# Average pooling of a 3D tensor: another cut of the rows into partitions, and one ring buffer for all loads

## The chip, the core and the metric

The kernel runs on one core of a Trainium2 chip. The metric is the device time of one execution in microseconds, as the median of several runs. Most runs of one kernel lie within a fraction of a per cent of each other.

## The reference

The input `x` is float32 of shape (8, 32, 32, 32, 32): 256 channels (batch times channel), each a cube of 32 x 32 x 32. With kernel size 2 every cube of 2 x 2 x 2 is replaced by its mean:

```
result[:, :, i, j, k] = mean(x[:, :, 2i:2i+2, 2j:2j+2, 2k:2k+2], axis=(-3, -2, -1))
```

The output is (8, 32, 16, 16, 16). 33.55 MB are read and 4.19 MB are written, and each input is used once. One *plane pair*, two neighbouring planes of 32 x 32 along the depth, is 2048 floats (8 KB) of contiguous memory and gives one output plane of 16 x 16, 256 floats (1 KB). There are 4096 such pairs, and in memory they follow each other without a gap, in the output too.

## The kernel before

`pool_rows` works on 128 partitions. The 256 channels are taken as two halves, `t` = 0 and 1: partition p holds channel p of the half. A channel is 128 KB of input and 16 KB of output, so rows of neighbouring partitions lie 128 KB apart in the input and 16 KB apart in the output. `KF` is 256 floats, 1 KB; positions and lengths in the code (`k0`, `kb`) count in KB per partition.

`plan` (L42) lists the loads. There are six of 32 KB per partition (4 MiB for all partitions), and the last two entries are cut into two loads of 16 KB each, so ten in all. Each entry takes a `tin` tile of 32 KB per partition out of a pool of five (L36, L72). All loads are issued by the sync engine (SP) at L77, in order, on one queue; the sixth and later ones wait until VectorE (DVE) is through with the tile that they overwrite. The first load is moved by hand ahead of the opening barrier of the program.

`pool_unit` (L53) runs on DVE, once for every part of an entry, ten times in all. It adds the two planes of each pair (L58, in place), then neighbouring columns (L62), then neighbouring rows with a scaling by 0.125 (L65, a tensor_tensor_reduce; its reduced result goes to `dummy` and isn't used). The result stays in SBUF, in `obuf[0]` and `obuf[1]`, 16 KB per partition each.

The stores come last (L85 to L89), on the same SP queue, behind all loads:

```
for t, k0, kb in [(0, 0, 16), (1, 0, 14), (1, 14, 2)]:
    nc.sync.dma_start(
        out=ov[t * P:(t + 1) * P, k0 * KF:(k0 + kb) * KF],
        in_=obuf[t][:, k0 * KF:(k0 + kb) * KF],
    )
```

The first holds the whole of half 0 (2 MiB), the second 14 of the 16 output planes of half 1 (1.75 MiB), the third the last two (256 KiB). Each waits for the DVE units that fill it. `tile_avg_pool_3d_kernel` then rewrites the closing of the program so that the closing barrier and the clearing of the other semaphores don't wait for the stores; only SP waits for them, at the very end.

Of the kernel before, what the change touches and what calls it, by code (L numbers as in the profile page):

```python
# [1 line left out]

# [4 lines left out]

F32 = mybir.dt.float32
KF = 256


@with_exitstack
def pool_rows(
    ctx: ExitStack,
    tc: tile.TileContext,
    x: bass.AP,
    kernel_size: int,
    out: bass.AP,
):
    nc = tc.nc  # L20
    assert kernel_size == 2, "only kernel_size == 2 supported"

    B, C, D, H, W = x.shape
    P = nc.NUM_PARTITIONS
    assert (B * C, D, H, W) == (2 * P, 32, 32, 32)
    add = mybir.AluOpType.add

    xv = x.rearrange("b c d h w -> (b c) (d h w)")  # L30
    ov = out.rearrange("b c d h w -> (b c) (d h w)")

    pool_in = ctx.enter_context(tc.tile_pool(name="pin", bufs=5))  # L36
    pool_out = ctx.enter_context(tc.tile_pool(name="pout", bufs=1))
    obuf = [pool_out.tile([P, 16 * KF], F32, name=f"obuf{t}") for t in range(2)]
    dummy = pool_out.tile([P, 1], F32, name="dummy")


    plan = [  # L42
        (0, 0, (32,)),
        (0, 32, (32,)),
        (0, 64, (32,)),
        (0, 96, (32,)),
        (1, 0, (32,)),
        (1, 32, (32,)),
        (1, 64, (16, 16)),
        (1, 96, (16, 16)),  # L50
    ]

    def pool_unit(buf, t, k0, kb):  # L53

        od = kb // 8
        a = buf.rearrange("p (o dd e) -> p o dd e", o=od, dd=2)
        b = buf[:, :od * 1024]
        nc.vector.tensor_add(  # L58
            out=b.rearrange("p (o e) -> p o e", o=od), in0=a[:, :, 0], in1=a[:, :, 1])
        bv = b.rearrange("p (e ww) -> p e ww", ww=2)  # L60
        c = buf[:, od * 1024:od * 1536]
        nc.vector.tensor_add(out=c, in0=bv[:, :, 0], in1=bv[:, :, 1])  # L62
        cv = c.rearrange("p (j hh k) -> p j hh k", hh=2, k=16)
        o0 = k0 * KF // 8
        nc.vector.tensor_tensor_reduce(  # L65
            out=obuf[t][:, o0:o0 + od * 256].rearrange("p (j k) -> p j k", k=16),
            in0=cv[:, :, 0], in1=cv[:, :, 1],
            scale=0.125, scalar=0.0, op0=add, op1=add, accum_out=dummy[:, :],
        )

    for t, k0, parts in plan:
        tin = pool_in.tile([P, 32 * KF], F32, tag="tin", name="tin")  # L72
        views = []
        o = 0
        for kb in parts:
            v = tin[:, o * KF:(o + kb) * KF]
            nc.sync.dma_start(  # L77
                out=v, in_=xv[t * P:(t + 1) * P, (k0 + o) * KF:(k0 + o + kb) * KF])
            views.append((v, k0 + o, kb))
            o += kb  # L80
        for v, k, kb in views:
            pool_unit(v, t, k, kb)


    for t, k0, kb in [(0, 0, 16), (1, 0, 14), (1, 14, 2)]:  # L85
        nc.sync.dma_start(
            out=ov[t * P:(t + 1) * P, k0 * KF:(k0 + kb) * KF],
            in_=obuf[t][:, k0 * KF:(k0 + kb) * KF],
        )  # L89


def kernel(tc: tile.TileContext, x: bass.AP, kernel_size: int, out: bass.AP):
    nc = tc.nc
    pool_rows(tc, x, kernel_size, out)
    tc.close()
    tc.compile()  # L96
    blocks = nc.main_func.blocks

    opening, program = blocks[0].instructions, blocks[tc.starting_block_idx].instructions
    load = next(i for i in program if isinstance(i, mybir.InstDMACopy))
    assert load.engine == nc.sync.engine
    barrier = next(
        n for n, i in enumerate(opening)
        if i.engine == load.engine and isinstance(i, mybir.InstDrain))
    program.remove(load)
    opening.insert(barrier, load)

    closing = blocks[-1].instructions
    stores = [
        i for i in program
        if isinstance(i, mybir.InstDMACopy) and "out_" in i.outs[0].memref]
    kept = [u.id for i in stores for u in i.sync_info.on_update]
    final = next(
        i for i in closing
        if i.engine == nc.sync.engine and isinstance(i, mybir.InstDrain))  # L120
    waits = {w.id: w for w in final.sync_info.on_wait}
    closing[closing.index(final)] = mybir.InstDrain(
        name=final.name, engine=final.engine, ins=[], outs=[], is_reset_sema=False,
        sync_info=mybir.SyncInfo(
            on_wait=[w for n, w in waits.items() if n not in kept], on_update=[]))


    reset = next(
        n for n, i in enumerate(closing)
        if isinstance(i, mybir.InstDrain) and i.is_reset_sema)  # L130
    first, stop = closing[reset].reset_range_start, closing[reset].reset_range_stop
    assert isinstance(closing[reset + 1], mybir.InstISA)
    while len(closing) > reset:
        closing.pop()
    n = first
    while n < stop:
        m = n
        while m < stop and m not in kept:
            m += 1
        if m > n:  # L140
            closing.append(mybir.InstDrain(
                name=nc.get_next_instruction_name(), engine=nc.gpsimd.engine, ins=[], outs=[],
                is_reset_sema=True, reset_range_start=n, reset_range_stop=m))
            nc.gpsimd.sem_clear(range(n, m))
        n = m + 1
    for n in kept:
        w = waits[n]
        closing.append(mybir.InstEventSemaphore(
            name=nc.get_next_instruction_name(), engine=nc.sync.engine, ins=[], outs=[],
            sync_info=mybir.SyncInfo(  # L150
                on_wait=[w],
                on_update=[mybir.SyncUpdate(
                    sync_type="semaphore", id=n, ant_name=w.ant_name,
                    update_mode="sem-sub-imm", update_value=w.wait_value)])))


# [1 line left out]
_INS = ['x', 'kernel_size']  # L158
_OUTS = [((8, 32, 16, 16, 16), 'float32')]

_NUMBERS = {'kernel_size': 2}


# [26 lines left out]
```

## Time and profile before

| what | value |
|---|---|
| median of 5 runs | 91.85 us (91.64 to 92.31) |
| the profiled execution: its own time | 91.68 us |
| the profiled execution: its span | 86.3 us |
| DVE busy | 64.0 us (74% of the span) |
| DMA queue, share of 16 engines | 99.4% |

The span runs from the first to the last instruction. Transfers that are still under way when the last instruction ends lie outside it, as do the start and the end of the execution; that is why its own time is longer. "Busy tenths" cut the span into 40 slices, one digit each, where 9 is 90% or more. In a group of instructions, the columns after the bar are busy time in us, mean ns of one, and the idle time just before them with what ended it. In the list of DMA issues the last column is the time from issue to landing. SPq in the timeline is SP's queue of DMA issues; the times there are start and duration in us.

### The profile page before, as it was taken

The numbers are of one execution on the slowest core, as the hardware profiler recorded it, in microseconds if no ns is written. First come the engines' busy times: TensorE is split into PE (matmuls) and PEld (weight loads), VectorE is DVE, ScalarE is ACT, GpSimd is POOL, SyncE is SP. The second block draws the span as 40 slices with busy tenths as digits, with TensorE's granted clock in tenths as the row PEclk, the third lists the DMA queues.
The fourth block names the chain that finished last, engine by engine and source line by source line (L and its number), as shares of the span: only waits on it lengthen the run. The fifth ranks groups of instructions, "written<-read, shape, count | busy, mean of one in ns | idle before, by whom it ended". The sixth has DMA issues, their size and how long they took to land.

```text
span 86.3 us, 90 instructions
## 1 busy us (share of the span) xinstructions
DVE 64.0 (74%) x40; POOL 0.2 (0%) x4
## 2 busy tenths in 40 slices
DVE  0000049992999749992999749992999999999994
POOL 0000000000000000000000000000000000000000
DMA  8959998899979999799988999698999999999999
GB/s 243 471 258 486 486 486 380 349 486 486 471 304 441 486 486 425 304 486 486 486 349 380 486 486 456 273 486 380 471 387 463 418 433 425 425 425 357 425 456 404
DMA packets 1639, 36.44 MB, mean 422 GB/s; under 512 B 176, under 2 KB 176, under 8 KB 176
## 3 DMA queue, kind: packets, MB, share of 16 engines
q1 hardware_dynamic: 1639, 36.44, 99.4%
HBM read 33.55 MB, written 4.19 MB: 438 GB/s over the span
## 4 chain that ended last, share of the span: by engine, by line
DMA 61%; DVE 37%; issue 0%; DVEq 0%
DMA tin<-in_x_dram 61%; DVE tin L58 21%; DVE tin L62 11%; DVE obuf L65 6%; DVE dummy L65 0%; DVEq L96 0%
## 5 line engine op out<-in xcount | busy, mean ns | idle before, releaser
L58 DVE TENSOR_TENSOR tin<-tin 128x4096 f32<-128x4096 f32 (+1 forms) x10 | 35.7, 3570 | 20.5 <-DMA tin<-in_x_dram 20.5
L62 DVE TENSOR_TENSOR tin<-tin 128x2048 f32<-128x2048 f32 (+1 forms) x10 | 18.6, 1865 | 0.3
L65 DVE CUSTOM_DVE_ANT_1 obuf<-tin 128x1024 f32<-128x1024 f32 (+1 forms) x10 | 10.1, 1011 | 0.3
L65 DVE DVE_READ_ACCUMULATOR2_ANT dummy<- 128x1 f32 x10 | 0.8, 82 | 0.0
L171 POOL MEMSET const-bfloat16-1.0<- 128x1 bf16 x1 | 0.1, 102 | 0.0
L171 POOL MEMSET const-uint8-127<- 128x1 uint8 x1 | 0.1, 102 | 0.0
L171 POOL MEMSET const-float32-0.0<- 128x1 f32 x1 | 0.1, 99 | 0.2 <-issue 0.2
L171 POOL MEMSET const-float32-1.0<- 128x1 f32 x1 | 0.1, 99 | 0.0
## 6 DMA issues: line engine op xcount, KB each, us to landing
tin<-in_x_dram SPq DMA_DIRECT2D x6, 4096.0 KB, 34.8
tin<-in_x_dram SPq DMA_DIRECT2D x4, 2048.0 KB, 38.0
out_dram<-obuf SPq DMA_DIRECT2D x1, 2048.0 KB, 36.2
out_dram<-obuf SPq DMA_DIRECT2D x1, 1792.0 KB, 8.9
out_dram<-obuf SPq DMA_DIRECT2D x1, 256.0 KB, 5.1
```

What stands on the lines that cost most here:

```text
L58: nc.vector.tensor_add(out=b.rearrange("p (o e) -> p o e", o=od), in0=a[:, :, 0], in1=a[:, :, 1])
L62: nc.vector.tensor_add(out=c, in0=bv[:, :, 0], in1=bv[:, :, 1])
L65: nc.vector.tensor_tensor_reduce(out=obuf[t][:, o0:o0 + od * 256].rearrange("p (j k) -> p j k", k=16), in0=cv[:, :, 0], in1=cv[:, :, 1], s ...
L171: nc = _bacc.Bacc("TRN2", target_bir_lowering=False, num_devices=1)
```

## The change

The halves are given up. The 4096 plane pairs are cut into two *regions*: the first 31 x 128 pairs, of which each partition takes 31 consecutive ones (248 KB of input, 31 KB of output), and the last 128 pairs, of which each takes one (8 KB and 1 KB). A partition's row no longer begins with a channel, and neighbouring rows lie 248 KB (31 KB in the output) apart.

The five tiles become one `ring` of 160 KB per partition, and `obuf` becomes one tile of 32 KB. A load now names its place in the ring (`r0`). There are eight loads instead of ten: one of 64 KB per partition (8 MiB), five of 32 KB, one of 24 KB and one of 8 KB, the last from the second region. The 64 KB load is worked on as two units of 32 KB, so there are nine units. The first instruction of each unit is held in program order. The three stores have 24, 7 and 1 KB per partition, the last from the second region. The computation of a unit, SBUF use, the engines and the single queue stay as they are.

```
-    xv = x.rearrange("b c d h w -> (b c) (d h w)")
-    ov = out.rearrange("b c d h w -> (b c) (d h w)")
-    pool_in = ctx.enter_context(tc.tile_pool(name="pin", bufs=5))
-    pool_out = ctx.enter_context(tc.tile_pool(name="pout", bufs=1))
-    obuf = [pool_out.tile([P, 16 * KF], F32, name=f"obuf{t}") for t in range(2)]
+    xf = x.rearrange("b c d h w -> (b c d h w)")
+    of = out.rearrange("b c d h w -> (b c d h w)")
+    regions = []
+    done = 0
+    for pairs in (31, 1):
+        n = P * pairs
+        regions.append((
+            xf[done * 8 * KF:(done + n) * 8 * KF].rearrange("(p f) -> p f", p=P),
+            of[done * KF:(done + n) * KF].rearrange("(p f) -> p f", p=P)))
+        done += n
+    pool = ctx.enter_context(tc.tile_pool(name="ring", bufs=1))
+    ring = pool.tile([P, 160 * KF], F32, name="ring")
+    obuf = pool.tile([P, 32 * KF], F32, name="obuf")
     plan = [
-        (0, 0, (32,)),
-        (0, 32, (32,)),
-        (0, 64, (32,)),
-        (0, 96, (32,)),
-        (1, 0, (32,)),
-        (1, 32, (32,)),
-        (1, 64, (16, 16)),
-        (1, 96, (16, 16)),
+        (0, 0, 64, 0),
+        (0, 64, 32, 64),
+        (0, 96, 32, 96),
+        (0, 128, 32, 128),
+        (0, 160, 32, 0),
+        (0, 192, 32, 32),
+        (0, 224, 24, 64),
+        (1, 0, 8, 88),
     ]
+    stores = [
+        (0, 0, 24),
+        (0, 24, 7),
+        (1, 0, 1),
+    ]
+    column = [sum((31, 1)[:r]) for r in range(2)]
...
-        nc.vector.tensor_add(
+        first = nc.vector.tensor_add(
             out=b.rearrange("p (o e) -> p o e", o=od), in0=a[:, :, 0], in1=a[:, :, 1])
+        tc.keep_in_program_order(first)
...
-    for t, k0, parts in plan:
-        tin = pool_in.tile([P, 32 * KF], F32, tag="tin", name="tin")
...
+    for r, k0, kb, r0 in plan:
         nc.sync.dma_start(
-            out=ov[t * P:(t + 1) * P, k0 * KF:(k0 + kb) * KF],
-            in_=obuf[t][:, k0 * KF:(k0 + kb) * KF],
+            out=ring[:, r0 * KF:(r0 + kb) * KF],
+            in_=regions[r][0][:, k0 * KF:(k0 + kb) * KF])
+        for o in range(0, kb, 32):
+            n = min(kb - o, 32)
+            pool_unit(ring[:, (r0 + o) * KF:(r0 + o + n) * KF],
+                      column[r] + (k0 + o) // 8, n)
+    for r, k0, kb in stores:
+        c = column[r] + k0
+        nc.sync.dma_start(
+            out=regions[r][1][:, k0 * KF:(k0 + kb) * KF],
+            in_=obuf[:, c * KF:(c + kb) * KF],
         )
```

## The prediction

> **What bounds the kernel now.** I read the profile page first: its DMA lines say how full the transfer engines are, and the groups of instructions say what VectorE (DVE) waits for.
>
> ```profile
> span 86.3 us, 90 instructions
> ...
> DVE  0000049992999749992999749992999999999994
> ...
> DMA  8959998899979999799988999698999999999999
> ...
> q1 hardware_dynamic: 1639, 36.44, 99.4%
> HBM read 33.55 MB, written 4.19 MB: 438 GB/s over the span
> ...
> L58 DVE TENSOR_TENSOR tin<-tin 128x4096 f32<-128x4096 f32 (+1 forms) x10 | 35.7, 3570 | 20.5 <-DMA tin<-in_x_dram 20.5
> ```
>
> The one DMA queue is 99.4% busy for the whole span; DVE has holes, all 20.5 us of them because input has not arrived. Then the timeline, where each DVE start after a hole marks the landing of a load:
>
> ```profile
> 0.00 40.24 SPq L77 DMA_DIRECT2D tin<-in_x_dram  x10
> ...
> 11.98 4.43 DVE L58 TENSOR_TENSOR tin<-tin 128x4096 f32<-128x4096 f32 x1 [11.98 <-DMA tin<-in_x_dram]
> 16.44 2.29 DVE L62 TENSOR_TENSOR tin<-tin 128x2048 f32<-128x2048 f32 x1
> 18.76 1.22 DVE L65 CUSTOM_DVE_ANT_1 obuf<-tin 128x1024 f32<-128x1024 f32 x1
> ...
> 21.69 4.43 DVE L58 TENSOR_TENSOR tin<-tin 128x4096 f32<-128x4096 f32 x1 [1.70 <-DMA tin<-in_x_dram]
> ...
> 31.40 4.42 DVE L58 TENSOR_TENSOR tin<-tin 128x4096 f32<-128x4096 f32 x1 [1.69 <-DMA tin<-in_x_dram]
> ...
> 85.03 0.08 DVE L65 DVE_READ_ACCUMULATOR2_ANT dummy<- 128x1 f32 x1
> ```
>
> Loads of 4 MiB land every 9.71 us (21.69 - 11.98, 31.40 - 21.69): 432 GB/s. A DVE unit on one of them takes about 7.95 us and then waits 1.7. Last, the DMA issues:
>
> ```profile
> out_dram<-obuf SPq DMA_DIRECT2D x1, 2048.0 KB, 36.2
> out_dram<-obuf SPq DMA_DIRECT2D x1, 1792.0 KB, 8.9
> out_dram<-obuf SPq DMA_DIRECT2D x1, 256.0 KB, 5.1
> ```
>
> SP issues the three stores at 49.16, 80.94 and 85.14 (issue records of the timeline), so they land at 85.4, 89.8 and 90.3. The first sat 36 us in the queue behind loads; the last also found the queue full. The packet records of the trace agree: each of the 16 engines moves packets without a gap from 1.00 us until at the latest 89.93. The time is therefore not set by the 86.3 us span (which ends with instructions) but by **the sum of all packets on an engine**: 1.0 us to the first packet, about 88.9 us of packets, and about 1.75 us after them make the 91.68 us of the profiled execution. That execution is 0.17 us below the median of the runs, 91.85.
>
> **What the Trainium skill says.** The page "DMA: Bandwidth & Descriptors", section "Where 436 GB/s comes from", puts the ceiling of the 16 ports at 435.2 GB/s; the 432 GB/s here is within 1% of it, so the trace agrees and leaves a better memory layout nearly nothing to win. The same page, "Queues, rings and completion order", has each engine take its ring's descriptors in order; the 36.2 us store shows that. Its section "Latency and other measured facts" lists copies that slow down at power-of-two row pitches: 207 GB/s at 512 KiB against 214 at full rate, cured by padding. Before has pitches of 128 KB (load) and 16 KB (store), below that list, and its loads run at the ceiling: no sign of such a loss.
>
> **The change, part by part.**
>
> *Packets.* One row of a partition is one packet. The trace gives 1.213 us for 32 KB, 0.611 for 16 KB, 0.535 for 14 KB and 0.084 for 2 KB: about 37.7 ns per KB and 7.5 to 9 ns per packet. Each engine serves 8 of the 128 partitions. Before: 48 packets of 32 KB (58.2 us), 40 of 16 KB (24.4), 8 of 14 KB (4.3), 8 of 2 KB (0.7), sum 87.6 us; the rest of the 88.9 is 0.6 us of slow first packets, 0.35 us of slow packets round 77.5 us, small scatter and semaphore writes. After, by the same two terms: 8 of 64 KB (19.3), 40 of 32 KB (48.5), 16 of 24 KB (14.6), 8 of 8 KB (2.5), 8 of 7 KB (2.2), 8 of 1 KB (0.4). The bytes are the same; 104 packets become 88, 16 x 7.5 to 9 ns = **-0.12 to -0.14 us**. Two DMAs fewer (13 to 11) save two 9 ns semaphore writes, -0.02. A 64 KB packet has not been seen; if each is cut in two, the gain is 0.06 smaller. I take **-0.15**.
>
> *Pitch of 248 KB (input) and 31 KB (output), tail rows of 8 and 1 KB.* Not in the trace. From below: the engines are at 432 of 435 GB/s, so at most 0.7% of 77.7 us of loads, 0.5 us, could be won, and most of that is the packet cost already counted. From above: the skill's nearest case, 207 against 214, is 3.4%, 2.6 us on the loads. I take zero, since 248 KB isn't a power of two and the slower side needs lock-step on one part of memory.
>
> *First load of 8 MiB.* DVE starts when both halves are in, at 21.69 (before's second landing), not 11.98. It is hidden: DVE had 20.5 us of idle time. Back-to-back units of 7.95 us follow (two in the first load), and loads land at 31.4, 41.1, 50.8, 60.5, 70.26, so units 1 to 6 end at 29.6, 37.6, 45.5, 53.5, 61.4, 69.4; unit 7 waits for its load, 70.26 to 78.2. The unit of 24 KB lies between the 7.95 us unit of 32 KB and the 4.20 us unit of 16 KB (72.43 to 76.63 in the timeline): 6.1 us, to 84.3. The unit of 8 KB, extrapolated, 2.3 us: DVE ends at **86.6**, 1.5 us later than the 85.1 of before.
>
> *Ring waits.* The loads into r0=0, 32, 64 wait for units 1, 2, 3 (29.6, 37.6, 45.5); 88 goes out right behind 64. Behind the waiting load on SP stand only later loads and stores. At these moments the queue holds loads that last until 50.8, 60.5 and 70.3, so each wait has over 20 us of cover: zero.
>
> *Stores.* 24 KB rows can be issued at 69.4, ten us before the last load is in (about 80): covered by loads. The 7 KB rows go at 84.3, while the 24 KB ones (7.3 us) run until about 87.6: covered. The 1 KB rows go at 86.7; with the 1.0 us that the first load took from issue to its first packet they are ready at 87.7. The earliest engine is through with the 7 KB rows at about 88.9 (it began on the 2 KB rows at 88.76 before): 1.2 us of cover. Zero. The closing barrier and the clearing of semaphores on POOL, 1.2 us after DVE's end before (85.1 to 86.3), move to 87.8 and stay hidden behind the stores, which land near 90.1.
>
> Sum: 91.68 - 0.15 = 91.53 against the profiled execution, **91.70 against the median**. A comparison of this kernel can tell about 0.5%, 0.46 us; this stays inside it.
>
> **The rivals.**
>
> *A, slower: the new addresses or the 64 KB packets move slower.* Place: the 77.7 us of loads. For it: neither is in the trace, and the slow first packets (1.8 to 2.0 us for 32 KB) show that memory can hold engines up. Against it: after the first packet, even before's power-of-two pitch ran at the port ceiling. It decides once a 32 KB packet takes over 1.223 us (0.46 + 0.15 us over the 64 such packets' worth of loads per engine). At the skill's 3.4% it gives 94.3 us; 1% gives 92.5. Chance 0.15.
>
> *B, slower: the last store comes too late.* It needs a DVE end beyond 87.8. From 21.69 on DVE has only 0.9 us of idle time left, so units 3.4% slower would do it; 5% slower (3.2 us, less 0.9 and 1.2) gives 92.8. All ten units of before keep the same durations within 1%, so 0.03.
>
> *C, faster: a disturbance of the old layout goes.* Round 77.5 us all engines have some slow packets, together 0.35 us per engine. If the pitch causes it, the result is 91.35, and with the slow first packets gone too 90.75. Nothing ties either to the pitch, and one execution can't show whether it returns. Chance 0.17 of going beyond 0.5%.
>
> *D, the packets are cut differently and nothing else shows*: 91.75, within the main case.
>
> **How the numbers follow.** Main case with D, 0.65: 91.70, and 91.4 to 92.0 with the scatter of the runs (91.64 to 92.31). C 0.17 below, A and B 0.18 above. Leaving out about 0.08 of C and 0.09 of A and B, the range is 91.2 to 92.5.
>
> **What would show it.** Right: the queue still over 99% busy, second 32 KB landing 9.71 us after the one before, first DVE start at 21.7, DVE busy almost without a hole after it, ending at 86.6; the span grows to about 87.8 while the time stands; the last store lands near 90.1. Wrong: loads more than 9.79 us apart (A); a last store that lands only some 2 to 3 us after its issue, with the engines empty before it (B); DMA ending before 89.4 (C); SP stalled on a ring wait with less than a load in the queue.

## The result, and the profile after

The changed kernel is slower by a third of a per cent: 92.25 us (median of 43 runs) against 91.94 (80 runs), ratio **1.0033, 95% interval 1.0023 to 1.0043**. The forecast was 0.15 us faster, the measurement is 0.31 us slower: 0.46 us apart, and the sign is wrong. The time lies inside the range of 91.2 to 92.5 us, which is owed to the width of that range and not to the account behind it. The difference stays inside the 0.5% that the prediction named, but with this many runs it is clear of noise. The changed kernel also scatters more: half of its runs lie between 92.04 and 92.52 us, half of before's between 91.83 and 92.09.

The page of the changed kernel:

```profile
span 88.2 us, 82 instructions
...
DVE  0000000000999999999999999999999699999994
...
DMA  9479999995998899998999998999998998999989
...
q1 hardware_dynamic: 1364, 37.19, 99.0%
HBM read 33.55 MB, written 4.19 MB: 428 GB/s over the span
...
L76 DVE TENSOR_TENSOR ring<-ring 128x4096 f32<-128x4096 f32 (+2 forms) x9 | 35.5, 3947 | 23.0 <-DMA ring<-in_x_dram 23.0
```

The bound is the same as before: the DMA queue is full. DVE idles first and then works almost without a hole. The timeline shows where that begins and ends (start, duration, engine, line, operation, and in brackets the idle time before it):

```profile
22.07 4.42 DVE L76 TENSOR_TENSOR ring<-ring 128x4096 f32<-128x4096 f32 x1 [22.07 <-DMA ring<-in_x_dram]
...
30.00 4.42 DVE L76 TENSOR_TENSOR ring<-ring 128x4096 f32<-128x4096 f32 x1
...
70.63 4.43 DVE L76 TENSOR_TENSOR ring<-ring 128x4096 f32<-128x4096 f32 x1 [0.89 <-DMA ring<-in_x_dram]
...
86.96 0.08 DVE L83 DVE_READ_ACCUMULATOR2_ANT dummy<- 128x1 f32 x1
```

The first load is awaited until 22.07, not 21.7; everything behind it is late by the same 0.4 us (70.63 for 70.26, DVE's end at 87.0 for 86.6, span 88.2 for 87.8). The stores, in the list of DMA issues (KB of each and time from issue to landing):

```profile
out_dram<-obuf SPq DMA_DIRECT2D x1, 3072.0 KB, 18.1
...
out_dram<-obuf SPq DMA_DIRECT2D x1, 896.0 KB, 5.3
out_dram<-obuf SPq DMA_DIRECT2D x1, 128.0 KB, 3.3
```

The last one is issued at 87.07 and lands at 90.36. In each profiled execution of the two kernels the time is that landing plus 1.39 or 1.40 us, so the landings are enough to do the account.

One profile is one execution, and this one (91.75 us) was quicker than the median. Below, each kernel is profiled three times. "First 64 KB" is the moment at which the first 64 KB of every partition have landed, by the landing records of the trace.

| execution | time | first 64 KB | from there to the last load | to the last store |
|---|---|---|---|---|
| before | 91.68 | 21.67 | 58.80 | 9.81 |
| before, second | 92.07 | 21.66 | 59.20 | 9.82 |
| before, third | 91.75 | 21.81 | 58.72 | 9.83 |
| changed | 91.75 | 22.04 | 58.57 | 9.75 |
| changed, second | 92.23 | 22.18 | 58.90 | 9.76 |
| changed, third | 92.40 | 22.31 | 58.94 | 9.75 |

The means (21.71, 58.91, 9.82 and 22.18, 58.80, 9.75) differ by +0.46, -0.10 and -0.07, together +0.29 us; the medians of the runs differ by 0.31. **The changed kernel loses 0.46 us before the first load is in, and gets 0.17 us back behind it.** Fewer packets can explain only a part of the 0.17. Of the 16 packets that each engine saves, eight lie in the first 64 KB and eight in the later loads, 0.06 to 0.07 us each time by the prediction's price; the stores have 24 packets per engine in both kernels. And the middle stretch differs by up to 0.48 us between executions of one kernel.

A load has landed when the last of the 16 engines is through with its share. The trace has 16 landing records for each transfer, read here as one for each engine. Averaged over the engines and the three executions:

| all times in us | before | changed |
|---|---|---|
| first 64 KB, average engine | 21.50 | 21.68 |
| first 64 KB, last engine | 21.71 | 22.18 |
| last store, average engine | 90.19 | 90.12 |
| last store, last engine | 90.44 | 90.73 |

The average engine ends 0.07 us *earlier* than before. What makes the kernel slower is how far the engines are apart: at the first 64 KB the first and the last of them differ by 0.25 to 0.50 us before and by 0.62 to 0.89 in the changed kernel, and in the three executions of each they stay apart to the last store (0.40 to 0.47 and 0.59 to 1.08 us).

### The profile page after: what moved, and what is told of

Same layout as the page of the kernel before. It is cut to its first block, busy times and chain, and to the rows that moved or that the text cites. A ratio compares the mean times of both kernels' runs of the same rounds, so it can differ in the third digit from the quotient of the medians.

```text
span 88.2 us, 82 instructions
## 1 busy us (share of the span) xinstructions
DVE 63.5 (72%) x36; POOL 0.2 (0%) x4
## 4 chain that ended last, share of the span: by engine, by line
DMA 62%; DVE 36%; issue 0%; DVEq 0%
DMA ring<-in_x_dram 62%; DVE ring L76 20%; DVE ring L81 11%; DVE obuf L83 6%; DVE dummy L83 0%; DVEq L111 0%
## 5 line engine op out<-in xcount | busy, mean ns | idle before, releaser
L76 DVE TENSOR_TENSOR ring<-ring 128x4096 f32<-128x4096 f32 (+2 forms) x9 | 35.5, 3947 | 23.0 <-DMA ring<-in_x_dram 23.0
L81 DVE TENSOR_TENSOR ring<-ring 128x2048 f32<-128x2048 f32 (+2 forms) x9 | 18.5, 2055 | 0.3
L83 DVE CUSTOM_DVE_ANT_1 obuf<-ring 128x1024 f32<-128x1024 f32 (+2 forms) x9 | 10.0, 1107 | 0.3
```

Of the source, the lines that this page charges most:

```text
L76: first = nc.vector.tensor_add(out=b.rearrange("p (o e) -> p o e", o=od), in0=a[:, :, 0], in1=a[:, :, 1])
L83: nc.vector.tensor_tensor_reduce(out=obuf[:, o0 * KF:(o0 + od) * KF].rearrange("p (j k) -> p j k", k=16), in0=cv[:, :, 0], in1=cv[:, :, 1] ...
```

## The experiments

All ratios are to the kernel before on the same chip. Theory S: packets of 64 KB get going more slowly than packets of 32 KB. Rivals: P, the 248 KB pitch; T, the tail of 24, 8, 7 and 1 KB rows.

### The first load cut in two (e1_first32)

```
-        (0, 0, 64, 0),
+        (0, 0, 32, 0),
+        (0, 32, 32, 32),
```

> The changed kernel with its first load of 64 KB per partition cut into two loads of 32 KB (nine loads); pitch, ring, tail and stores stay. Theory S (the start: 64 KB packets on idle engines cost more than 32 KB packets): first load lands near 11.9 us and the second near 21.7 (not 22.07), ratio to before 0.998 to 1.000. Rivals P (the 248 KB pitch) and T (the tail of 24, 8, 7 and 1 KB rows): second landing still near 22.0 under P, 21.7 under T; the ratio stays near 1.003 under both.

Measured: 1.0004 (0.9992 to 1.0016), 91.90 us. Against the changed kernel that is -0.29%, and P and T are still in place, so neither alone makes the loss in the time. The landings didn't come as S had them, though. Timeline of this kernel:

```profile
12.33 4.42 DVE L77 TENSOR_TENSOR ring<-ring 128x4096 f32<-128x4096 f32 x1 [12.33 <-DMA ring<-in_x_dram]
...
22.01 4.43 DVE L77 TENSOR_TENSOR ring<-ring 128x4096 f32<-128x4096 f32 x1 [1.66 <-DMA ring<-in_x_dram]
```

The first 32 KB are 0.35 us later than the 11.98 us of before and the second 0.3 later: the pitch has a part in the landings. (This execution, of 92.06 us, was one of the longer ones of its kernel.)

### 32 KB first, 64 KB second (e3_second64)

```
-        (0, 0, 64, 0),
-        (0, 64, 32, 64),
+        (0, 0, 32, 0),
+        (0, 32, 64, 32),
```

> The changed kernel with the first two loads in the other order of size: 32 KB per partition first, then 64 KB. S: the 64 KB packets now come when the engines are already moving, and cost nothing; both have landed near 31.4, ratio 0.998 to 1.000. If 64 KB packets are slow wherever they stand, or under P or T: landing near 31.8, ratio 1.003.

Measured: 1.0003 (0.9992 to 1.0014). The same packets in another order, 0.30% quicker than the changed kernel: 64 KB packets are harmless once the engines move. The second load landed at 31.63, between the two figures expected; in e1, with packets of 32 KB throughout, the same 96 KB were in at 31.70.

### 8 KB first (e4_first8)

```
-        (0, 0, 64, 0),
+        (0, 0, 8, 0),
+        (0, 8, 24, 8),
+        (0, 32, 32, 32),
```

> The changed kernel with its first 64 KB per partition cut into loads of 8, 24 and 32 KB. If what is lost at the start grows with the size of the first packet (0.6 us for 32 KB, 0.8 and more for 64 KB by the packet records), an 8 KB packet loses about 0.15 to 0.3: the 64 KB have landed near 21.3, and the ratio is 0.994 to 0.997, faster than both. If the loss is a fixed time of the first accesses whatever their size: landing near 21.7, ratio 0.998 to 1.000. Under P and T: 1.003.

Measured: 1.0012 (1.0002 to 1.0023), first 64 KB at 21.84. A miss: 21.3 was expected. The start gains at most 0.15 us over e1, and the time shows no gain at all. A loss in proportion to the first packet is ruled out. (e4 has eight packets per engine more than e1, 0.06 to 0.07 us by the prediction's price, which would cover the 0.08% between the two.)

### Before's pitch, first load of 64 KB (e2_pitch128, e6_pitch128_first32)

Two regions of 16 pairs (128 KB), last loads of 24 and 8 KB, stores of 16, 15 and 1 KB; e6 cuts the first load in two besides.

```
-    for pairs in (31, 1):
+    for pairs in (16, 16):
...
-        (0, 128, 32, 128),
-        (0, 160, 32, 0),
-        (0, 192, 32, 32),
-        (0, 224, 24, 64),
-        (1, 0, 8, 88),
+        (1, 0, 32, 128),
+        (1, 32, 32, 0),
+        (1, 64, 32, 32),
+        (1, 96, 24, 64),
+        (1, 120, 8, 88),
...
```

> The changed kernel with the pitch of before: two regions of 16 plane pairs (128 KB), the first load still 64 KB per partition, the last loads 24 and 8 KB, stores of 16, 15 and 1 KB. S: no help, first load lands near 22.0, ratio about 1.003 or more. P: first load lands near 21.7, ratio 0.998 to 1.000. T: like the changed kernel in the ratio, 1.003, with the first landing at 21.7.

> The kernel with the changed tail at the pitch of before (loads of 24 and 8 KB, stores of 16, 15 and 1 KB) and a first load of 32 KB. Its sister with a first load of 64 KB lost about 1.1 us per engine after 76 us, against 0.35 to 0.5 elsewhere, and had a ratio of 1.0048. If that is the tail (8 KB rows that lie 128 KB apart, or the store behind them): second landing near 21.7, last load landed near 81.1, ratio 1.002 to 1.004. If it was one unlucky execution and the first load made the 1.0048: ratio 0.999 to 1.001.

Measured: e2 1.0048 (1.0034 to 1.0063), first 64 KB at 21.83; e6 1.0035 (1.0021 to 1.0049), second landing at 21.69. Both starts are better than the changed kernel's, and both are slower than before all the same. Their last loads land at 81.17 and 81.03, 10.8 and 10.7 us after the load that lands at 70.4 and 70.3; in the three profiles of the changed kernel that stretch takes 10.0 to 10.4 us. So they don't answer the question: something at their end costs as much as what was looked for. By the packet records it is mostly slow packets in the last loads, 0.9 and 0.8 us per engine against 0.3 to 0.5. Against each other, 64 KB first and 32 KB first, the two differ by 0.13%, which is within the noise (about 0.2% by the two intervals).

### Before's pitch, changed tail (e7_pitch128_tail, e8_pitch128_tail_first32)

Three regions, with pitches of 128, 120 and 8 KB; the 8 KB rows at the end are contiguous, as in the changed kernel. e8 has a first load of 32 KB. The loads name the regions accordingly.

```
-    for pairs in (31, 1):
+    for pairs in (16, 15, 1):
...
-        (0, 0, 24),
-        (0, 24, 7),
-        (1, 0, 1),
+        (0, 0, 16),
+        (1, 0, 15),
+        (2, 0, 1),
```

> The changed kernel with only its main pitch altered: three regions of 16, 15 and 1 plane pairs (pitches 128, 120 and 8 KB), so that the first load (64 KB) has the pitch of before, while the last loads (24 KB, and 8 KB contiguous) and the last store stay as in the changed kernel; stores of 16, 15 and 1 KB. If the loss needs the 248 KB pitch and the 64 KB packets together at the start: first landing near 21.9, ratio 0.997 to 0.999, as for the kernel with before's tail. If 64 KB rows at the start cost whatever the pitch (S as first put): 1.002 to 1.004. If the changed tail costs 0.3%: 1.001 to 1.003 with a last load landing near 81.

> The same with the first 64 KB cut into two loads of 32 KB. Second landing near 21.7. If the size of the first packet matters at the pitch of before as well, this is faster than its sister by 0.2 to 0.3%; if only together with the 248 KB pitch, the two agree within 0.1%.

Measured: 1.0043 (1.0029 to 1.0058) and 1.0036 (1.0022 to 1.0051). The two differ by 0.07%, as expected if size alone does nothing at this pitch; but the two intervals leave about 0.2% of room, so a smaller cost of size isn't excluded. Why both are slow is in the windows of e7 (start and end, length, DVE busy, POOL busy, TensorE clock, share of the 16 DMA engines in use, GB/s) and in its timeline:

```profile
82.00:84.00 2.00, 1.97 (x2) 0.00 (x0) 1.00 1.05 451
84.00:86.00 2.00, 1.97 (x4) 0.00 (x0) 1.00 0.69 295
86.00:87.80 1.80, 1.01 (x3) 0.00 (x0) 1.00 0.98 410
```

```profile
84.74 2.67 SPq L101 DMA_DIRECT2D out_dram<-obuf  x2
```

From 84 to 86 us the engines are used to 69% only. The 15 KB store needs DVE's unit of 24 KB and is issued at 84.74, as the 16 KB store runs out. The packet records give 0.5 us of idle time per engine there in e7, 0.3 in e8, 0.1 in e2 and e6, and none in the changed kernel, whose 24 KB store lasts until 87.3. It is what rival B of the prediction feared for the last store, here at the store before it. Besides, the last loads have 0.7 us of slow packets per engine in both, against 0.3 to 0.5 in the changed kernel.

### The same with the store split (e11_pitch128_split_store)

```
-        (1, 0, 15),
+        (1, 0, 12),
+        (1, 12, 3),
```

> The kernel with main pitches of 128 and 120 KB and the changed kernel's contiguous tail (first load 64 KB) again, with its 15 KB store cut into 12 and 3 KB, so that 12 KB rows can be issued near 78 us. In the first form the 15 KB store was issued at 84.7 us, only as the 16 KB store before it ran out; the engines were idle for 0.5 us there (packet records, 84 to 86 us), and that spoiled the comparison. If the loss of the changed kernel needs the 248 KB pitch together with 64 KB packets at the start: no idle engines after 84 us, ratio 0.997 to 1.000. If a 64 KB first load costs at any pitch, or the contiguous 8 KB tail costs: 1.002 to 1.004 in spite of the full queue.

The window and the timeline's line of the stores:

```profile
84.00:86.00 2.00, 1.97 (x4) 0.00 (x0) 1.00 0.96 408
```

```profile
78.57 8.73 SPq L102 DMA_DIRECT2D out_dram<-obuf  x3
```

The queue stays full (0.96 of the engines from 84 to 86 us, the 12 KB store issued at 78.57), and the ratio falls from 1.0043 to 1.0011 (0.9999 to 1.0023). That lies between the two ranges expected. Set against the changed kernel, with which it shares the size of every load, it is 0.22% quicker (0.06 to 0.38%, by the two intervals): with the pitch of 128 KB two thirds of the loss are gone, by the middle of the interval, although the first load is of 64 KB. The first load landed at 21.96 us.

### Before's pitch and tail, one 64 KB load, first or second (e5_before_first64, e9_pitch128_second64)

Two regions of 16 pairs, last four loads of 16 KB and stores of 16, 14 and 2 KB, as before; what differs from before is the ring, the order in which DVE's first instructions are held, and the joined load. The loads of e5, with the regions of e2:

```
        (0, 0, 64, 0),
        (0, 64, 32, 64),
        (0, 96, 32, 96),
        (1, 0, 32, 128),
        (1, 32, 32, 0),
        (1, 64, 16, 32),
        (1, 80, 16, 48),
        (1, 96, 16, 64),
        (1, 112, 16, 80),
```

e9 has `(0, 0, 32, 0), (0, 32, 64, 32)` for its first two.

> The pitch, the tail and the stores of before (two regions of 16 plane pairs; last four loads of 16 KB; stores of 16, 14 and 2 KB), in the ring, with only the first two loads joined to one of 64 KB per partition. S: the first load lands at 21.9 or later (21.67 is before's second landing, 21.83 and 21.90 were seen with 64 KB at this pitch), ratio 1.002 to 1.004. If the start costs only when 64 KB packets and the 248 KB pitch come together: ratio 0.999 to 1.001.

> The kernel with pitch, tail and stores of before and one 64 KB load (ratio 0.9982 with that load first), now with 32 KB first and 64 KB second. At 248 KB the same exchange gave -0.30%. If size and pitch act together: no difference to 0.9982 beyond 0.1%. If 64 KB packets cost at the start whatever the pitch: 0.995 to 0.997.

Measured: e5 **0.9982 (0.9972 to 0.9992)**, faster than both kernels; e9 0.9997 (0.9981 to 1.0013). At 128 KB a first load of 64 KB shows no cost in the time, and taking it out of the first place wins nothing; at 248 KB the same exchange won 0.30%. By the times, S as first put, a cost of 64 KB packets at any start, falls, and the loss needs size and pitch together (the joint theory from here on). Of the gain of e5, 0.17 us, eight packets per engine fewer than before explain 0.06 to 0.07; the rest is open.

The landing in e5 speaks the other way:

```profile
21.93 4.43 DVE L77 TENSOR_TENSOR ring<-ring 128x4096 f32<-128x4096 f32 x1 [21.93 <-DMA ring<-in_x_dram]
```

By the landing records the first load was in at 21.91 us, as S had it, and 0.2 us later than before's first 64 KB (21.71). This execution won that back between the first load and the last (58.68 us).

### The start by itself (m1_idle_starts248, m2_idle_starts128)

Every load goes to the same place of the ring, so it waits for DVE and begins on idle engines, with no other load queued behind it. m1, at 248 KB (m2, at 128 KB, has loads of 64, 32, 32, 64, 32 and 32 KB):

```
-        (0, 64, 32, 64),
-        (0, 96, 32, 96),
-        (0, 128, 32, 128),
-        (0, 160, 32, 0),
-        (0, 192, 32, 32),
-        (0, 224, 24, 64),
-        (1, 0, 8, 88),
+        (0, 64, 32, 0),
+        (0, 96, 64, 0),
+        (0, 160, 32, 0),
+        (0, 192, 32, 0),
+        (0, 224, 24, 0),
+        (1, 0, 8, 0),
```

> The cost by itself, several times in one execution: the changed kernel with all loads into the same place of the ring (r0 = 0), so that each waits until DVE is through with the one before and starts on idle engines; sizes in order 64, 32, 64, 32, 32, 24, 8 KB per partition. The time as a whole tells nothing. If packets of 64 KB get going more slowly on any idle engines: every 64 KB load takes from issue to landing over 9.9 us longer than a 32 KB one (9.70 by the steady rate; 22.04 - 11.96 = 10.08 between the changed kernel and before). If only the first access of an execution is slow: the 64 KB load in third place is 9.70 longer than the 32 KB loads beside it, and the later 32 KB loads take less than the 11.96 us of before's first.

> The same with the pitch of before (two regions of 16 plane pairs): sizes 64, 32, 32, 64, 32, 32 KB. If the 248 KB pitch makes starts slower (rival P, for the start alone), loads of one size and place take some 0.2 us less here than with 248 KB; if not, the same within 0.1 us.

The idle time of DVE before a unit shows these loads. First m1, then m2:

```profile
21.95 4.43 DVE L75 TENSOR_TENSOR ring<-ring 128x4096 f32<-128x4096 f32 x1 [21.95 <-DMA ring<-in_x_dram]
42.30 4.42 DVE L75 TENSOR_TENSOR ring<-ring 128x4096 f32<-128x4096 f32 x1 [4.41 <-DMA ring<-in_x_dram]
72.27 4.42 DVE L75 TENSOR_TENSOR ring<-ring 128x4096 f32<-128x4096 f32 x1 [21.95 <-DMA ring<-in_x_dram]
...
113.97 4.43 DVE L75 TENSOR_TENSOR ring<-ring 128x4096 f32<-128x4096 f32 x1 [13.34 <-DMA ring<-in_x_dram]
```

```profile
21.92 4.42 DVE L74 TENSOR_TENSOR ring<-ring 128x4096 f32<-128x4096 f32 x1 [21.92 <-DMA ring<-in_x_dram]
41.94 4.43 DVE L74 TENSOR_TENSOR ring<-ring 128x4096 f32<-128x4096 f32 x1 [4.07 <-DMA ring<-in_x_dram]
62.02 4.42 DVE L74 TENSOR_TENSOR ring<-ring 128x4096 f32<-128x4096 f32 x1 [12.05 <-DMA ring<-in_x_dram]
...
93.16 4.43 DVE L74 TENSOR_TENSOR ring<-ring 128x4096 f32<-128x4096 f32 x1 [23.12 <-DMA ring<-in_x_dram]
```

From issue to landing, 32 KB loads take 12.28 and 12.28 us at 248 KB, and 11.95, 12.00, 11.96 and 11.95 us at 128 KB: **the pitch alone costs an idle start of 32 KB 0.32 us.** The first loads of whole kernels agree: 12.30 and 12.29 us in e1 and e3, 11.95 to 12.14 in the six kernels and repeats with 32 KB first at 128 KB (three of them before). (The second 32 KB load waits only 4.41 and 4.07 us, because DVE still works on the second half of the 64 KB load when it is issued.) Loads of 64 KB take 21.93 and 21.89 us at 248 KB, and 21.90 at 128: here the pitch makes no difference. Neither S nor the joint theory said that. The two loads with 13.34 and 23.12 us of idle time are a find of another kind, told at the end.

### The start with a load queued behind (m3_starts248_followed, m4_starts128_followed)

m3 puts a load of 16 KB, with a place of its own, behind each load of 64 KB. m4 does so twice at 128 KB; two loads of 48 KB follow. The loads of m3:

```
         (0, 0, 64, 0),
...
+        (0, 64, 16, 64),
+        (0, 80, 64, 0),
+        (0, 144, 16, 64),
+        (0, 160, 64, 0),
+        (0, 224, 16, 64),
...
```

> Idle starts again, 248 KB pitch: loads of 64 KB that begin on idle engines, each with a load of 16 KB queued behind it (the earlier idle starts had nothing behind them and took 21.9 us in both pitches; the changed kernel took 22.07 to 22.3). The time as a whole tells nothing. If a load queued behind makes the slowest engine later: 22.1 to 22.4 from issue to landing for each; if not, 21.9.

> The same at the pitch of before (two regions of 16 pairs), two starts of 64 KB with 16 KB behind. If pitch and size act together: 21.8 to 21.95 here and 22.1 or more at 248 KB; if size alone with a follower: 22.1 or more here too.

m3, and after it m4:

```profile
22.28 4.42 DVE L75 TENSOR_TENSOR ring<-ring 128x4096 f32<-128x4096 f32 x1 [22.28 <-DMA ring<-in_x_dram]
```

```profile
21.88 4.42 DVE L73 TENSOR_TENSOR ring<-ring 128x4096 f32<-128x4096 f32 x1 [21.88 <-DMA ring<-in_x_dram]
```

The first load of the execution took 22.26 us at 248 KB and 21.86 at 128, as the joint theory has it. The later 64 KB starts took 21.84 and 21.73 us in m3 and 21.88 in m4, all without loss. But those starts don't test what they were built for. SP's queue in m3, for the second load of 64 KB and the 16 KB load behind it:

```profile
38.26 0.33 SPq L89 DMA_DIRECT2D ring<-in_x_dram  x1
...
42.46 0.33 SPq L89 DMA_DIRECT2D ring<-in_x_dram  x1
```

The follower had to wait for DVE to free its own place, and was issued 4.2 us after the load that it should stand behind (so too at the third start, 76.11 and 80.31, and in m4, 37.86 and 42.06). The first packets of that load began 1.0 to 1.7 us after its issue, so they had nothing queued behind them. Only the first load of an execution had a follower in time, at 0.79 us. Whether a load queued behind has a part in the loss is therefore open, and the figures would allow it: at 248 KB the first 64 KB load took 22.04, 22.18, 22.31 and 22.26 us with a load queued behind it, and 21.93 in m1, where nothing was. At 128 KB, first loads of 64 KB took 21.83 to 21.96 us in five of six executions, with a load behind or (m2) without, and 22.06 in e7.

### Both kernels again (a2_again, a3_again, b2_before_again, b3_before_again)

> The changed kernel once more, unchanged, for a second profile: its profiled execution of 91.75 us lies well below the median of 92.25. S: the landing of the first load varies from execution to execution, and this one, if its time is nearer 92.25, has it later than 22.07, by about as much as the time is longer. Rivals: the first load lands at 22.0 again and a longer time comes from the tail, after 77 us.

> The changed kernel a third time, unchanged; as the second look.

> The kernel before once more, for a second profile. S: second landing within 0.1 us of 21.67, and if the execution is longer than 91.68 the difference lies after 70 us (last load landed later than 80.47).

> The kernel before a third time, unchanged. As in the second look: S has the second landing within 0.1 us of 21.67, and what a longer execution adds lies after 70 us.

The third execution of the changed kernel, and the third of before:

```profile
22.34 4.42 DVE L76 TENSOR_TENSOR ring<-ring 128x4096 f32<-128x4096 f32 x1 [22.34 <-DMA ring<-in_x_dram]
```

```profile
12.15 4.43 DVE L58 TENSOR_TENSOR tin<-tin 128x4096 f32<-128x4096 f32 x1 [12.15 <-DMA tin<-in_x_dram]
21.84 4.43 DVE L58 TENSOR_TENSOR tin<-tin 128x4096 f32<-128x4096 f32 x1 [1.66 <-DMA tin<-in_x_dram]
```

The six executions are those of the table above. The changed kernel's first landing moves between 22.04 and 22.31 and makes up some 0.3 us of the 0.65 us between its shortest and longest profile; the rest is between the first load and the last, and varies in before too (58.72 to 59.20). S, for the second look, had the whole difference at the start; it was a third of it. For before it had the second landing within 0.1 us of 21.67; the third execution, at 21.81, misses that.

With these, the records give the first 64 KB in 17 executions (mean, and number of executions; e4, with 8 KB first at 248 KB, had 21.84):

| first 64 KB in, us | pitch 128 KB | pitch 248 KB |
|---|---|---|
| two loads of 32 KB | 21.74 (5) | 21.99 (1) |
| one load of 64 KB | 21.92 (6) | 22.14 (5) |

By the landings, rows of 64 KB cost about 0.2 us, the pitch costs about 0.2 us, and the two add up. By the times only both together cost anything: e1 and e3 have the pitch alone, e5 the size alone, and none of them shows a loss. A single execution scatters by 0.2 to 0.4 us within one field of this table, so it isn't settled which of the two is right.

## Why the prediction was wrong

- **Packets: the prices are right, the gain is not shown.** 104 packets became 88. A 64 KB row is one packet of 2.418 us, the value worked out from the two terms. The 24, 8, 7 and 1 KB packets take 0.912, 0.309, 0.272 and 0.046 us by the records, as worked out to within 2 ns. Half of the saved packets belong to the first 64 KB, where the loss swallowed them. Behind it about 0.08 us were due and 0.17 were measured: 0.10 between the first load and the last, which three executions each can't tell from noise, and 0.07 in the stores, where no packet is saved.
- **First load: the step that failed.** "DVE starts when both halves are in, at 21.69 (before's second landing)". The sum took the start of before over as it was: "1.0 us to the first packet" and "0.6 us of slow first packets", the same for all 16 engines. Neither is a constant, and the engines are not alike. By the packet records of the first profiles, the engines begin on average 0.14 us after the 1.0 us mark in before and 0.29 us in the changed kernel, and lose 0.63 and 0.77 us to slow packets until 4.5 us. The last engine's first packet begins at 1.70, 1.45 and 1.43 us in the three executions of before and at 2.27, 1.80 and 1.98 in those of the changed kernel; already in before "without a gap from 1.00 us" held for the earliest engines only. The first 64 KB landed at 22.18 on average for 21.71: the missing term is +0.46, for which the sum had zero. That DVE's late start is hidden was right, but the same delay lies on the DMA queue, where nothing hides it.
- **Pitch and 64 KB packets, rival A: half right, in the wrong place.** Steady packets of 32 KB take 1.213 us at either pitch, so the test that it named, loads over 9.79 us apart, stays negative (9.72 us). The cost sits in the first packets alone. The prediction had the evidence, slow first packets of 1.8 to 2.0 us, and used it for the rival's sign, but priced the rival as a slower rate of all loads and not as a slower start.
- **Ring waits and stores: right.** The loads into used places are issued at 30.1 to 46.3 us, with more than 20 us of queue ahead; the last store finds the queue full. Rival B, a late last store, did not come in the changed kernel, but four of the experiments met its like with a 15 KB store issued at 84.5 to 84.7 us.
- **The Trainium skill's row on pitches** (page "DMA: Bandwidth & Descriptors", section "Latency and other measured facts") lists large powers of two, from 512 KiB up, as row pitches at which copies lose rate. The prediction took zero for the pitch because 248 KB isn't a power of two. Here a pitch of 31 x 8 KB makes a start of 32 KB slower (12.28 us) than one of 128 KB (11.96); for the start of a load, of which the row doesn't speak, the measurement decides, and a pitch that isn't a power of two is no safeguard. For steady streams, of which it speaks, no run here contradicts the page.

Shown: the loss lies before the first load is in, with the engines that get through last. At this pitch it goes from the time when the first packets are of 32 KB (1.0004, 1.0003). At 128 KB a kernel with a 64 KB first load shows no loss (0.9982), and with the changed tail about two thirds of the loss go (1.0011).

Not settled: whether size and pitch cost something each, as the landings have it, or only together, as the times have it; whether a load queued behind has a part; why memory or engines give the first packets a slower start; and why later 64 KB starts at the same pitch don't show it.

## What to carry to other kernels

When a kernel is bound by a full DMA queue, count its packets, but give the start a price of its own: the first packets are slow, what they cost changed here with row size and pitch, and nothing hides it. Look at the last engine and not only at the average. Begin with rows of a size that has been measured at the pitch in use, and put larger ones after them (at 248 KB, 32 KB first did well; 8 KB first won nothing more). Issue each store while the one before it has still more than a microsecond to run: from issue to first packet a load took 1.0 us here. To place a difference of 0.3%, profile each kernel several times: one execution differs from the next by as much as the change does.

## What the hardware showed that was not expected

- **A store queued right behind a load makes that load land a microsecond later.** In m1 a 32 KB load with a store behind it took 13.28 us from issue to landing and its two sisters 12.28; in m2 a 64 KB load took 23.07 and its sister 21.90. These are two cases; the slow packets begin between 2.4 and 4.7 us before the load's end. All the complete kernels show such packets at 77 to 80 us, before their first store begins, with 0.3 to 0.9 us lost per engine; they vary from execution to execution, and nothing here shows what sets their size.
- **Engines don't start together.** The first packets of an execution begin between 1.0 and 2.4 us after the first issue, and the last of the 16 engines sets the landing.
- **Packets are very regular in between:** 1.213 us for 32 KB, at both pitches, within 1% in the changed kernel from 22 to 70 us.
